# A hidden layer of gates as a block product of seven parts

## The chip, the cores and the metric

The kernel runs on one core of a Trainium2 chip. The metric is the device time of one execution in microseconds, here the median of the runs shown; one execution was also taken by the profiler, with its own time.

## The reference

Two layers over 512 latent tokens of width 1024, in float32, with 256 context tokens beside them in the first layer. Each layer normalizes, modulates with a scale and a shift made from a conditioning vector, mixes tokens, projects back and adds a gated residual. The first mixer is a bidirectional gated recurrence of 16 heads of 128 channels:

```python
    p = (h @ w_in).reshape(B, N, HG_STREAMS, HG_HEADS, HG_HEAD_DIM)
    q = jax.nn.silu(p[0])
    f = lbh + (1.0 - lbh) * jax.nn.sigmoid(p[1:3].astype(jnp.float32))
    return q, 1.0 - f, jnp.log(f), p[3], p[4]
```

So a head has five streams: a query, two forget gates (one for each direction), a value and a gate path. The context goes through the same weights and gives the state with which the latent recurrence of each direction starts; of a context token only the gates and the value are needed. The second mixer is a Fourier transform over tokens and channels, with its own gate path. A last normalization ends it.

## The kernel before

A product in float32 is made of three matmuls on rounded parts: `mm3` multiplies high by high, high by low and low by high. The parts of the tokens (`hlh`, `hll` for latent, `hc` for context, 8 blocks of 128 channels each) are made once. Those of the weights are made as they arrive: `split` copies the high part on ScalarE (ACT, L56, `wh`) and subtracts it on VectorE (DVE, L57, `wl`). The class `Weights` keeps three raw tiles of 512 KB (`wr`, fetched by SyncE, SP) and three of each part, and works one piece ahead of the product.

A head's streams 1 and 2 are the gates, 0 the query and 3 the gate path. `proj` makes for each gate 24 matmuls of 512 latent columns (`pf`) and 24 of 256 context columns (`pfc`), then 24 of 512 for the query and 24 for the path (both `pq`). The gate's sigmoid and its scale run on ACT (L455, L456), its complement goes to the tile `z` (L466). `proj_v` makes the values of two heads (`vps`, matmuls of 256 columns). The program goes through eight pairs: `proj` of the even head, `proj_v`, `proj` of the odd head.

Beside it runs the recurrence of the head before (`scan`): seven levels that double the span. At each level after the first, four matmuls `gp` (L578, eight with both passes of float32) go from `z` and its copy `kk` into PSUM; DVE multiplies `z` twice by the decays (L586), ACT makes the next `kk` (L545), and DVE copies the masked scores (L605). The next `gp` needs this `kk`. After the levels come the states, the read-out, its normalization (POOL, GpSimd) and the head's output `y`, kept in SBUF (`py`). `advance` runs one piece of a scan at each yield of the projections, and from step 30 on every third step runs a piece of the side work `ada_rest`: 32 loads of 512 KB (`ar`, two buffers, the next requested ahead of the use) that DVE accumulates (L401) into rows, from which come the second layer's modulation and two residual gates (`gates`, in SBUF).

Inside the startup the order of PE, ACT and DVE is that of the program (`manual_schedule`); POOL and SP are free. For each of eight blocks d it makes modulation columns (`rp`, `row` on ACT, then the matmul `mp`), transposes the latent tokens, modulates them into `hlh` and `hll`, and runs products of head 0 between. Then it does the same for the context. Everywhere else a scheduler sets each engine's order, by priorities that follow the program and by the buffers that come free. At the end the output product of the first layer takes `y` of all heads (`out0_early`, `out0_late`), and the second layer follows.

## Time and profile before

| | us |
|---|---|
| median of the runs (lowest, highest) | 1210.17 (1208.92, 1210.5) |
| profiled execution | 1208.84 |
| its span, first to last instruction | 1207.0 |
| TensorE (PE) busy | 1186.8 (98%) |
| VectorE (DVE) busy | 763.6 (63%) |
| ScalarE (ACT) busy | 562.6 (47%) |
| GpSimd (POOL) busy | 42.8 (4%) |

The mean granted TensorE clock is 0.995. "PEld" is the weight load, which runs beside the matmuls. In a group's row stand the line, engine, operation, output and inputs with their shapes, then the count, busy time, the mean of one in ns, and the engine's idle time before them with what ended it. In a timeline's row the first two numbers are start and length in us.

### The profile page before, as it was taken

The numbers are of one execution on the slowest core, as the hardware profiler recorded it, in microseconds if no ns is written. First come the engines' busy times: TensorE is split into PE (matmuls) and PEld (weight loads), VectorE is DVE, ScalarE is ACT, GpSimd is POOL, SyncE is SP. The second block draws the span as 40 slices with busy tenths as digits, with TensorE's granted clock in tenths as the row PEclk, the third lists the DMA queues.
The fourth block names the chain that finished last, engine by engine and source line by source line (L and its number), as shares of the span: only waits on it lengthen the run. The fifth ranks groups of instructions, "written<-read, shape, count | busy, mean of one in ns | idle before, by whom it ended". The sixth has DMA issues, their size and how long they took to land.

```text
span 1207.0 us, 18983 instructions
## 1 busy us (share of the span) xinstructions
PE 1186.8 (98%) x7677; PEld 1050.8 (87%) x7677; DVE 763.6 (63%) x1250; ACT 562.6 (47%) x1130; POOL 42.8 (4%) x76
## 2 busy tenths in 40 slices
...
GB/s 358 183 123 141 71 53 53 53 71 70 168 59 31 174 78 53 71 140 71 36 70 53 35 54 70 37 53 107 163 179 182 111 43 134 108 108 120 88 87 70
DMA packets 33673, 118.52 MB, mean 98 GB/s; under 512 B 3879, under 2 KB 4144, under 8 KB 33586
## 3 DMA queue, kind: packets, MB, share of 16 engines
...
## 4 chain that ended last, share of the span: by engine, by line
PE 90%; DVE 4%; DMA 2%; ACT 2%; issue 1%; POOL 1%; SPq 0%; DVEq 0%; POOLq 0%; ACTq 0%
PE gp L578 7%; PE pf L95 4%; PE pq L95 4%; PE pq L97 4%; PE pq L96 4%; PE pf L97 4%; PE pf L96 4%; PE vps L95 4%; PE vps L96 4%; PE vps L97 4%; PE pfc L95 2%; PE pfc L96 2%; PE pfc L97 2%; PE o0a L97 2%; PE o0a L95 2%; PE o0a L96 2%
## 5 line engine op out<-in xcount | busy, mean ns | idle before, releaser
L56 ACT ACTIVATE wh<-wr 128x1024 fp32r<-128x1024 f32 x140 | 148.0, 1058 | 229.9 <-PE pq L96 89.3
L57 DVE TENSOR_TENSOR wl<-wr,wh 128x1024 fp32r<-128x1024 f32 x140 | 170.7, 1220 | 100.4 <-ACT wh L56 100.2
L586 DVE TENSOR_TENSOR z<-z,tt 128x512 f32<-128x512 f32 x192 | 124.0, 687 | 122.3 <-PE gp L578 110.9
L578 PE MATMUL gp<-z,kk 128*128 128x128 f32 x768 | 103.5, 277 | 0.7 <-ACT kk L545 0.6
L578 PEld LDWEIGHTS gp<-z,kk 128*128 128x128 f32 x768 | 97.6, 191 | 6.7 <-ACT kk L545 3.3
L95 PE MATMUL pf<-hlh,wh 128*128 128x512 f32 x240 | 99.2, 413 | 0.0
L95 PE MATMUL pq<-hlh,wh 128*128 128x512 f32 x240 | 97.1, 405 | 0.0
L545 ACT ACTIVATE kk<-z 128x512 f32<-128x512 f32 x96 | 61.8, 644 | 71.5 <-DVE z L586 71.3
L97 PE MATMUL pf<-hlh,wl 128*128 128x512 f32 x240 | 94.5, 394 | 0.0
L97 PE MATMUL pq<-hlh,wl 128*128 128x512 f32 x240 | 93.9, 391 | 0.0
L96 PE MATMUL pf<-hll,wh 128*128 128x512 f32 x240 | 93.7, 391 | 0.0
L96 PE MATMUL pq<-hll,wh 128*128 128x512 f32 x240 | 93.5, 390 | 0.0
L95 PE MATMUL pfc<-hc,wh 128*128 128x256 f32 x256 | 74.8, 292 | 0.0
L95 PE MATMUL vps<-wh,hlh 128*128 128x256 f32 x256 | 74.2, 291 | 0.0
L97 PE MATMUL vps<-wh,hll 128*128 128x256 f32 x256 | 72.6, 283 | 0.0
L96 PE MATMUL vps<-wl,hlh 128*128 128x256 f32 x256 | 72.5, 283 | 0.0
L96 PE MATMUL pfc<-hc,wh 128*128 128x256 f32 x256 | 72.4, 283 | 0.0
L97 PE MATMUL pfc<-hc,wl 128*128 128x256 f32 x256 | 72.4, 283 | 0.0
L97 PEld LDWEIGHTS pf<-hlh,wl 128*128 128x128 f32 x240 | 45.0, 188 | 10.4 <-issue 0.2
L97 PEld LDWEIGHTS pq<-hlh,wl 128*128 128x128 f32 x240 | 45.1, 188 | 10.0
L95 PEld LDWEIGHTS pf<-hlh,wh 128*128 128x128 f32 x240 | 45.2, 188 | 9.5 <-issue 1.9
L96 PEld LDWEIGHTS pf<-hll,wh 128*128 128x128 f32 x240 | 45.3, 189 | 8.2 <-issue 0.2
...
## 6 DMA issues: line engine op xcount, KB each, us to landing
wr<-hg_w SPq DMA_DIRECT2D x64, 512.0 KB, 3.5
ar<-ada_r SPq DMA_DIRECT2D x32, 512.0 KB, 3.8
wr<-ft_w SPq DMA_DIRECT2D x32, 512.0 KB, 4.0
wr<-hg_wout SPq DMA_DIRECT2D x29, 512.0 KB, 3.5
wa<-ada_a SPq DMA_DIRECT2D x16, 512.0 KB, 10.5
wr<-hg_v SPq DMA_DIRECT2D x16, 512.0 KB, 3.4
wr<-ft_wout SPq DMA_DIRECT2D x16, 512.0 KB, 3.5
xs<-x SPq DMA_DIRECT2D x4, 512.0 KB, 3.7
```

What stands on the lines that cost most here:

```text
L56: s.activation(hi, src, AF.Copy)
L57: v.tensor_tensor(out=lo, in0=src, in1=hi.bitcast(F32), op=ALU.subtract)
L95: pe.matmul(out, lh, rh, start=first, stop=False)
L96: pe.matmul(out, lh, rl, start=False, stop=False)
L97: pe.matmul(out, ll, rh, start=False, stop=last)
L545: s.activation(view(kk, 0, [[2 * h, T // (2 * h)], [h, 2], [1, h]]), view(z4, 2 * T, [[2 * h, T // (2 * h)], [T + h, 2], [1, h]]), AF.Copy)
L578: pe.matmul(gp[:, n * P:(n + 1) * P], kk[:, n * P:(n + 1) * P], view(z4, n * P, dims), start=True, stop=True)
L586: v.tensor_tensor(out=za, in0=za, in1=ta, op=ALU.mult)
```

## The change

The 2048 columns that a head's two gates make (two streams, latent and context) become one product of a weight matrix and a token matrix, each cut two by two. Weights are cut by stream and by half of the 1024 input channels, tokens by half of the channels and by even and odd blocks of 128 tokens (384 of the 768). Seven products of sums replace eight:

- `mixes` makes the four token sums with four dependent subtractions and additions on POOL for each k (256 latent columns, later 128 context columns), and splits each into high and low parts (ACT and DVE). This stands in the startup: latent k = 0 to 3 after the blocks d = 4 to 7, context after d = 5 and 7 of the context. The modulated tokens are written back into `xs` for it. The casts and sums of the masks on POOL now stand inside the startup too, and the mask tile has four planes.
- `fold_piece` makes the seven weight pieces of 128 x 512 out of the two streams' raw tiles, four of them by a DVE operation in place. Each is split.
- In `proj`, for heads 1 to 15, `prod` runs 12 matmuls of 384 columns for each piece (`px`). Five sums on DVE, two copies on ACT and two additions on POOL put the results together, and sigmoid and gate run on all 768 columns at once. Head 0 is as before.

To make room, the outputs `y` of heads 0 to 12 go to DRAM (`yd`) and come back in halves (`yr`) for the output product; the two residual gates go there as rows (`grow`) and come back broadcast. The side work's `ar` has one buffer, and the next load is requested behind the use of the one before.

```diff
--- before.py
+++ after.py
...
+    pd = ctx.enter_context(tc.tile_pool(name="pd", bufs=1, space=bass.MemoryType.DRAM))
...
-                if j == 3:
-                    hi, lo = (py.tile(shape, F32R, tag=f"yp{6 + b}", name=f"wz{b}") for b in range(2))
+                if j in pieces:
+                    both = pw.tile([P, 2, KT // 2, P], F32R, tag="wh" if pieces[j] % 2 else "wl", name=f"wp{j}")
+                    hi, lo = both[:, 0], both[:, 1]
+                elif j == 3:
+                    hi, lo = (p0.tile(shape, F32R, tag=f"junk{b}", name=f"wz{b}") for b in range(2))
...
-            self.halves(n + 1)
+            self.halves(n + 3 if n in pieces and pieces[n] < 4 else n + 1)
...
-        h32 = p0.tile([P, T], F32, tag="h32", name=f"h32_{d}_{e}", bufs=2)
+        h32 = xs[:, n0:n1, d * P:(d + 1) * P]
+        t3 = tp[:, :w].rearrange("p (n c) -> p n c", c=P)
...
+    def mixes(k0, k1, e):
+        m, n0 = ((2, 0), (1, NT))[e]
+        xt = xs.rearrange("p n (h k c) -> p h k n c", h=2, c=P)
+
+        def part(kh, half, k):
+            return xt[:, kh, k, n0 + half:n0 + half + 2 * m - 1:2, :]
+
+        for t in range(4):
+            if mix[t] is None:
+                mix[t] = [ph.tile([P, KT // 2, N // 2], F32R, tag=f"t{2 * t + b}", name=f"mix{t}_{b}") for b in range(2)]
+        for k in range(k0, k1):
+            b11, b12, b21, b22 = (part(kh, half, k) for kh in range(2) for half in range(2))
+            g.tensor_tensor(out=b22, in0=b22, in1=b12, op=ALU.subtract)
+            g.tensor_tensor(out=b12, in0=b12, in1=b11, op=ALU.subtract)
+            g.tensor_tensor(out=b11, in0=b22, in1=b11, op=ALU.add)
+            g.tensor_tensor(out=b21, in0=b21, in1=b11, op=ALU.subtract)
+            for t, src in ((2, b22), (0, b12), (1, b11), (3, b21)):
+                c = slice(0, 2 * P) if e == 0 else slice(2 * P, 3 * P)
+                hi, lo = (mix[t][b][:, k, c].rearrange("p (n c) -> p n c", c=P) for b in range(2))
+                split(hi, lo, src)
...
+    def fold_piece(w, j):
+        p = pieces[j]
+        w.loaded(j - p + 1)
+        f1, f2 = w.raw[j - p], w.raw[j - p + 1]
+        a11, a12, a21, a22 = f1[:, :4], f1[:, 4:], f2[:, :4], f2[:, 4:]
+        if p == 2:
+            v.tensor_tensor(out=a21, in0=a21, in1=a22, op=ALU.add)
+            v.tensor_tensor(out=a11, in0=a21, in1=a11, op=ALU.subtract)
+        elif p == 4:
+            v.tensor_tensor(out=a21, in0=a22, in1=a11, op=ALU.subtract)
+        elif p == 5:
+            v.tensor_tensor(out=a12, in0=a12, in1=a11, op=ALU.subtract)
+        return (a11, a12, a11, a21, a21, a12, a22)[p]
+
+    def head_specs(i):
+        if i == 0:
+            for st in (1, 2):
+                spec(("w", i, st), a["hg_w"][i, st], [P, KT, P])
+        else:
+            for p in range(7):
+                pieces[len(specs)] = p
+                spec(("f", i, p), a["hg_w"][i, 1 + p] if p < 2 else None, [P, KT, P], fold_piece)
+        for st in (0, 3):
+            spec(("w", i, st), a["hg_w"][i, st], [P, KT, P])
...
-            if d == 6:
-                W.halves(3)
+            if d >= KT // 2:
+                mixes(d - 4, d - 3, 0)
+        W.halves(3)
         for j in range(3):
             product(j, KT - 2)
         for n in range(NT, NT + NTC):
             normalize(n)
         for j in range(3):
             product(j, KT - 1)
+        g.tensor_copy(masks, mraw[:, 1:])
+        for t, src in ((own_m, ident), (near_m, mraw[:, 0, :])):
+            msum = p0.tile([P, 32], F32, tag="msum", name=f"msum{t.name}", bufs=2) if t is near_m else own_m
+            g.tensor_tensor(out=msum, in0=src[:, 0:32], in1=src[:, 32:64], op=ALU.add)
+            for j in (64, 96):
+                g.tensor_tensor(out=msum, in0=msum, in1=src[:, j:j + 32], op=ALU.add)
+            if t is near_m:
+                g.tensor_copy(near_m, msum)
...
+            if d in (5, 7):
+                mixes(d - 5, d - 3, 1)
...
+    yd = [pd.tile([P, T], F32, name=f"yd{i}") for i in range(13)]
...
-                raw = sp.tile([P, D], F32, tag="ar", name=f"ar{j}_{k}", bufs=2)
+                raw = sp.tile([P, D], F32, tag="ar", name=f"ar{j}_{k}")
...
-                fetch()
...
+                fetch()
...
-                    s.activation(gates[0 if j == 0 else 1][:, h * 512:(h + 1) * 512], q, AF.Copy)
+                    s.activation(acc[0:1, h * 512:(h + 1) * 512], q[0:1, :], AF.Copy)
+                nc.sync.dma_start(out=grow[0 if j == 0 else 1], in_=acc[0:1, :])
...
+        def out(st, half):
+            return ff[:, 2 - st].rearrange("p (n e c) -> p e n c", e=2, c=P)[:, half]
+
+        def tri(t):
+            return t[:, :nh].rearrange("p (n c) -> p n c", c=P)
+
+        def prod(p, rhs):
+            acc = psP(f"px{i}_{p}")
+            hi, lo = W.get(base + p)
+            for k in range(KT // 2):
+                mm3(tri(acc), hi[:, k, :], lo[:, k, :], rhs(0, k), rhs(1, k), k == 0, k == KT // 2 - 1)
+            return acc
+
+        def block(kh, half):
+            return lambda b, k: tiled[b][:, kh * 4 + k, half]
+
+        def mixed(t):
+            return lambda b, k: mix[t][b][:, k, :].rearrange("p (n c) -> p n c", c=P)
+
+        def kept(acc, name):
+            c = sp.tile([P, nh], F32, tag="cc", name=f"{name}{i}", bufs=2)
+            s.activation(c, acc[:, :nh], AF.Copy)
+            return c
+
+        def add(eng, dst, x, y):
+            eng.tensor_tensor(out=dst, in0=x, in1=y, op=ALU.add)
+
+        u = kept(prod(0, block(0, 0)), "u")
+        yield None
+        add(v, out(1, 0), tri(prod(1, block(1, 0))), tri(u))
+        yield None
+        add(v, u, prod(2, mixed(1))[:, :nh], u)
+        yield None
+        c5 = kept(prod(3, mixed(0)), "c5")
+        add(g, out(1, 1), tri(u), tri(c5))
+        yield None
+        add(v, u, prod(4, mixed(2))[:, :nh], u)
+        add(g, out(2, 1), tri(u), tri(c5))
+        yield None
+        add(v, out(1, 1), tri(prod(5, block(1, 1))), out(1, 1))
+        s.activation(ff[:, 1, :], ff[:, 1, :], AF.Sigmoid)
+        gate(1)
+        yield None
+        add(v, out(2, 0), tri(prod(6, mixed(3))), tri(u))
+        s.activation(ff[:, 0, :], ff[:, 0, :], AF.Sigmoid)
+        gate(2)
+        yield None
         for st, dst in ((0, q), (3, zs)):
...
+        y = py.tile([P, T], F32, tag="y" if i < LAST else f"y{i}", name=f"y{i}")
         v.scalar_tensor_tensor(out=y, in0=tp, scalar=ngc, in1=zs, op0=ALU.mult, op1=ALU.mult)
+        if i < LAST:
+            nc.sync.dma_start(out=yd[i], in_=y)
...
+    def y_fetch(k, r, ahead):
+        n = back[r].index((k, r))
+        for kk, _ in back[r][:n + 1 + ahead]:
+            if (kk, r) not in got:
+                t = got[kk, r] = (fp if r else sp).tile([P, 256], F32, tag="yr" if r else "cc", name=f"yr{r}_{kk}",
+                                                        bufs=3 if r else 2)
+                nc.sync.dma_start(out=t, in_=yd[kk][:, r * 256:(r + 1) * 256])
+        return got[k, r]
+
+    def y_parts(k, r, late=True):
+        y2 = (fp if late else sp).tile([P, 2, 256], F32R, tag="o0y" if late else "q", name=f"o0y{r}_{k}", bufs=2)
+        src = ys[k][:, r * 256:(r + 1) * 256] if k >= LAST else y_fetch(k, r, 2 if late else 1)
+        split(y2[:, 0], y2[:, 1], src)
...
+    for j in range(2):
+        gates[j] = fp.tile([P, D], F32, tag=f"gate{j}", name=f"gate{j}")
+        nc.sync.dma_start(out=gates[j], in_=grow[j].broadcast_to([P, D]))
```

In the startup, ACT, around the blocks d = 4 and 5 (`hlh` is the modulated block, `row` the copy of the next block's modulation row, `mix` the high parts of the token sums, `xs` the modulated block in float32). Before:

```order
L238 ACTIVATE hlh<-tp_0_378,bcol,acol 128x512
L215 ACTIVATE row_410<-rp_401 128x256
L238 ACTIVATE hlh<-tp_0_416,bcol,acol 128x512
L241 ACTIVATE h_5_0_436<-tp_0_416,bcol,acol 128x512
L215 ACTIVATE row_448<-rp_439 128x256
```

and in the change:

```order
L250 ACTIVATE hlh<-tp_0_376,bcol,acol 128x512
L58 ACTIVATE mix_0_402<-xs 128x256
L58 ACTIVATE mix_0_398<-xs 128x256
L58 ACTIVATE mix_0_400<-xs 128x256
L58 ACTIVATE mix_0_404<-xs 128x256
L227 ACTIVATE row_427<-rp_418 128x256
L250 ACTIVATE hlh<-tp_0_433,bcol,acol 128x512
```

Four copies of sums stand between a block's modulation and the next block's row.

In the pairs, DVE, at the levels of head 13 beside the gates of head 14 (`z` multiplications by `tt`, masked copies `am`, weight splits `wl` and `wp`, sums of the products `px`). Before:

```order
L586 TENSOR_TENSOR z_13_6571<-z_13_6571,tt_0_6908 128x2x128x2 x2
L605 COPY_PREDICATED am_6882<-masks,gp_1_6925 128x512
L586 TENSOR_TENSOR z_13_6571<-z_13_6571,tt_1_6935 128x2x64x4 x2
L605 COPY_PREDICATED am_6882<-masks,gp_2_6968 128x512
L57 TENSOR_TENSOR wl_7087<-wr_6865,wh_7086 128x1024
L513 SCALAR_TENSOR_TENSOR rr<-fc_6858,ones 128x255
L586 TENSOR_TENSOR z_13_6571<-z_13_6571,tt_2_6978 128x2x32x8 x2
L605 COPY_PREDICATED am_6882<-masks,gp_3_6999 128x512
L586 TENSOR_TENSOR z_13_6571<-z_13_6571,tt_3_7009 128x2x16x16 x2
L605 COPY_PREDICATED am_6882<-masks,gp_4_7032 128x512
```

and in the change:

```order
L686 TENSOR_TENSOR z_13_6871<-z_13_6871,tt_0_7214 128x2x128x2 x2
L705 COPY_PREDICATED am_7188<-masks,gp_1_7234 128x512
L574 TENSOR_TENSOR u_7184<-px_2_7250,u_7184 128x384
L59 TENSOR_TENSOR wl_7382<-wr_7318,wh_7381 128x1024
L686 TENSOR_TENSOR z_13_6871<-z_13_6871,tt_1_7244 128x2x64x4 x2
L705 COPY_PREDICATED am_7188<-masks,gp_2_7268 128x512
L686 TENSOR_TENSOR z_13_6871<-z_13_6871,tt_2_7278 128x2x32x8 x2
L705 COPY_PREDICATED am_7188<-masks,gp_3_7299 128x512
L574 TENSOR_TENSOR u_7184<-px_4_7317,u_7184 128x384
L59 TENSOR_TENSOR wl_7422<-wr_7347,wh_7421 128x1024
L686 TENSOR_TENSOR z_13_6871<-z_13_6871,tt_3_7309 128x2x16x16 x2
```

A sum of a product and a split now stand between the masked copy and the next multiplication at every second level.

In the side work, DVE, at one of its groups (`acc` accumulates `ar`). Before, with the multiplications of head 4:

```order
L399 TENSOR_SCALAR acc_2867<-ar_0_2600,scol 128x1024
L401 SCALAR_TENSOR_TENSOR acc_2867<-ar_1_2868,scol,acc_2867 128x1024
L586 TENSOR_TENSOR z_4_2186<-z_4_2186,tt_5_2859 128x2x4x64 x2
L401 SCALAR_TENSOR_TENSOR acc_2867<-ar_2_2976,scol,acc_2867 128x1024
L401 SCALAR_TENSOR_TENSOR acc_2867<-ar_3_3073,scol,acc_2867 128x1024
L57 TENSOR_TENSOR wl_3047<-wr_2831,wh_3046 128x1024
L401 SCALAR_TENSOR_TENSOR acc_2867<-ar_4_3124,scol,acc_2867 128x1024
L513 SCALAR_TENSOR_TENSOR rr<-fc_2824,ones 128x255
L401 SCALAR_TENSOR_TENSOR acc_2867<-ar_5_3251,scol,acc_2867 128x1024
```

and in the change, with those of head 6:

```order
L461 TENSOR_SCALAR acc_3822<-ar_0_3678,scol 128x1024
L686 TENSOR_TENSOR z_6_3303<-z_6_3303,tt_1_3806 128x2x64x4 x2
L705 COPY_PREDICATED am_3743<-masks,gp_2_3848 128x512
L463 SCALAR_TENSOR_TENSOR acc_3822<-ar_1_3941,scol,acc_3822 128x1024
L686 TENSOR_TENSOR z_6_3303<-z_6_3303,tt_2_3858 128x2x32x8 x2
L705 COPY_PREDICATED am_3743<-masks,gp_3_3885 128x512
L463 SCALAR_TENSOR_TENSOR acc_3822<-ar_2_4062,scol,acc_3822 128x1024
L686 TENSOR_TENSOR z_6_3303<-z_6_3303,tt_3_3895 128x2x16x16 x2
L705 COPY_PREDICATED am_3743<-masks,gp_4_3928 128x512
```

Three accumulations, each of a load that is requested behind the one before, stand between level multiplications; before, only the last multiplication had any of the group ahead of it.

164 lines of the change are left out of this document (76 added, 88 removed).

## The prediction

> **What bounds the kernel now.** I read the page's first part and its chain of waits, then the stretches of the span, then the timeline.
>
> ```profile
> PE 1186.8 (98%) x7677; PEld 1050.8 (87%) x7677; DVE 763.6 (63%) x1250; ACT 562.6 (47%) x1130; POOL 42.8 (4%) x76
> PE 90%; DVE 4%; DMA 2%; ACT 2%; issue 1%; POOL 1%; SPq 0%; DVEq 0%; POOLq 0%; ACTq 0%
> ```
>
> TensorE (PE) is busy for 98% and the chain runs on it for 90%: a matmul removed is time gained, as long as nobody else becomes late. The stretches say where somebody could (columns: stretch, its length, busy time and instructions of PE, PEld, DVE, ACT, POOL, the granted clock, DMA share, GB/s):
>
> ```profile
> 20.00:30.00 10.00, 8.07 (x50) 5.12 (x43) 4.90 (x10) 4.77 (x7) 0.00 (x0) 0.74 1.03 410
> 50.00:60.00 10.00, 7.33 (x36) 5.00 (x34) 7.25 (x14) 4.55 (x7) 4.88 (x8) 1.00 0.42 139
> 70.00:80.00 10.00, 10.00 (x92) 9.29 (x91) 10.00 (x17) 5.47 (x11) 0.00 (x0) 1.00 0.34 105
> 230.50:329.50 99.00, 98.65 (x663) 88.88 (x662) 65.29 (x103) 49.18 (x107) 2.86 (x4) 1.00 0.30 96
> 626.60:725.70 99.10, 99.10 (x682) 89.87 (x682) 58.24 (x99) 48.19 (x105) 2.40 (x4) 1.00 0.18 57
> ```
>
> The last two are pairs of heads: PE never stops, VectorE (DVE) has 58 of 99 us, 65 where the side work runs. The first three belong to the startup: PE has holes, and just after it DVE is full.
>
> **Gate matmuls (A).** Starts of neighbours give the pitch: 22 intervals of 512 columns between the first two rows, 22 of 256 between the last two.
>
> ```profile
> 421.87 0.39 PE L96 MATMUL pq<-hll,wh 128*128 128x512 f32 x1
> 426.86 0.39 PE L97 MATMUL pq<-hlh,wl 128*128 128x512 f32 x1
> 399.88 0.28 PE L96 MATMUL pfc<-hc,wh 128*128 128x256 f32 x1
> 402.51 0.28 PE L97 MATMUL pfc<-hc,wl 128*128 128x256 f32 x1
> ```
>
> That is 0.2268 and 0.1195 us. A head's gates were 48 of 512 and 48 of 256 columns, 16.62 us; now 7 products x 4 blocks x 3 = 84 of 384 columns. No row has 384; I take the middle, 0.1732, 14.55 us. So 2.07 us less for each of 15 heads: **-31.1 us**. Bounds: priced as 256 columns -98.7, as 512 columns +36.4.
>
> **What that costs the other engines in the pairs (B).** The groups:
>
> ```profile
> L57 DVE TENSOR_TENSOR wl<-wr,wh 128x1024 fp32r<-128x1024 f32 x140 | 170.7, 1220 | 100.4 <-ACT wh L56 100.2
> L57 DVE TENSOR_TENSOR o1y<-yf,o1y 128x512 fp32r<-128x512 f32 x16 | 10.9, 681 | 0.0
> L473 DVE TENSOR_TENSOR q<-pq,q 128x512 f32<-128x512 f32 x15 | 10.2, 683 | 0.0
> L57 DVE TENSOR_TENSOR u<-up,u 128x258 fp32r<-128x258 f32 x16 | 6.7, 418 | 0.0
> L56 ACT ACTIVATE wh<-wr 128x1024 fp32r<-128x1024 f32 x140 | 148.0, 1058 | 229.9 <-PE pq L96 89.3 <-issue 53.3 <-PE zp L96 25.4
> L56 ACT ACTIVATE o1y<-yf 128x512 fp32r<-128x512 f32 x16 | 9.9, 620 | 3.2 <-DVE u L57 2.8 <-PE dp L97 0.4
> L455 ACT ACTIVATE fl<-pf 128x512 f32<-128x512 f32 x30 | 17.9, 598 | 54.9 <-PE pf L97 54.8
> L455 ACT ACTIVATE fc<-pfc 128x256 f32<-128x256 f32 x32 | 11.8, 374 | 0.0
> L456 ACT ACTIVATE fl<-fl,lbc,omlb 128x512 f32<-128x512 f32 x32 | 26.0, 815 | 1.0
> L456 ACT ACTIVATE fc<-fc,lbc,omlb 128x256 f32<-128x256 f32 x32 | 19.1, 599 | 0.5
> ```
>
> DVE per head: two weight splits of 1024 go (-2.44), seven of 512 come (7 x 0.681 = 4.77), four folds (4 x 0.683 = 2.73), five adds of 384 columns (between 0.418 and 0.683, say 0.55: 2.75). Together +7.8, so a pair has 58 + 16 = 74, with side work 81, in the 95 us that PE leaves: 78% and 85%. ScalarE (ACT): seven copies of 0.620 for two of 1.058 (+2.2), two copies of 384 columns near 0.49, and the four gate steps on 768 columns (0.82 and 1.03 by the lines through 256 and 512) for eight (4.77 to 3.70, -1.1): +2.1, 52 of 95 us. Two additions per head go to GpSimd (POOL), beside other work.
>
> DVE is not full, so the cost is a loop. Levels of the recurrence run beside the products:
>
> ```profile
> 433.36 1.12 PE L578 MATMUL gp<-z,kk 128*128 128x128 f32 x8
> 434.23 0.38 PE L95 MATMUL pfc<-hc,wh 128*128 128x256 f32 x1
> 434.60 1.29 DVE L586 TENSOR_TENSOR z<-z,tt 128x512 f32<-128x512 f32 x2 [2.98 <-PE gp L578]
> 435.81 0.73 DVE L605 COPY_PREDICATED am<-masks,gp 128x512 f32<-128x512 uint8 x1
> 435.92 0.63 ACT L545 ACTIVATE kk<-z 128x512 f32<-128x512 f32 x1 [0.25 <-DVE z L586]
> ```
>
> One level's matmul at 433.36 makes the next possible at 435.92 + 0.63 = 436.55: 3.19 us round. PE had 0.87 (433.36 to 434.23) plus twelve matmuls of 512 or 24 of 256 columns to issue meanwhile, 3.6 to 3.7 us, so DVE sat waiting (the 2.98). Beside an odd head's levels PE now has one product, 0.87 + 12 x 0.1732 = 2.95 us: the round no longer fits and PE waits 0.24 us at each of six levels, 1.44 a pair. Three of these rounds have a copy (0.73), an addition (0.55) and a split of 1024 (1.22) in DVE's row between two multiplications (1.29): 3.79, or 0.84 late; but the rounds between them have only the copy and can make that up. So 1.4 for each of some 7 pairs that have both: **+10 us**. Bounds: 0 if products of which PE already has the operands lie ahead of the late level; 3 x 0.84 + 3 x 0.24 = 3.24 a pair, +24, if nothing is made up. I take the bare round, since the additions can slip behind the multiplications.
>
> **One buffer for the side work (C).**
>
> ```profile
> ar<-ada_r SPq DMA_DIRECT2D x32, 512.0 KB, 3.8
> L401 DVE SCALAR_TENSOR_TENSOR acc<-ar,scol,acc 128x1024 f32<-128x1024 f32 x30 | 38.4, 1280 | 10.0 <-DMA ar<-ada_r 9.9
> ```
>
> With two buffers the next load ran beside the accumulation and DVE still waited 9.9 us for loads. With one, a step takes 3.8 + 1.28 = 5.1 us. Three of the accumulations of each later group stand in DVE's row between level multiplications, beside PE rounds of 3.7 us: 3 x 1.4 = 4.2 per group, less the slack with which the first of them begins, about 3, for the three groups after the startup: **+9 us**. Head weights queue on SP behind these loads, with two to three tiles ahead to cover it. Bounds: 0 if DVE gets early, +27 if all seven reloads of a group count in full.
>
> **Startup (D).** Here ACT and DVE keep the written order, and PE was back to back:
>
> ```profile
> 40.90 0.50 PE L221 MATMUL mp<-sel,row 128*128 128x2 f32 x4
> 44.90 0.50 PE L221 MATMUL mp<-sel,row 128*128 128x2 f32 x4
> 38.45 0.38 ACT L215 ACTIVATE row<-rp 128x256 f32<-128x256 f32 x1
> 38.58 0.81 DVE L243 TENSOR_SCALAR h<-tp,acol,bcol 128x512 f32<-128x512 f32 x1 [0.91 <-ACT hlh L238]
> 2.69 0.25 POOL L361 TENSOR_TENSOR own_m<-ident 128x32 f32<-128x32 f32 x1 [1.62 <-DMA ident<-ident]
> 49.06 0.41 POOL L179 TENSOR_SCALAR rstd_x<-ss 128x1 f32<-128x1 f32 x1 [35.10 <-ACT junk L201]
> 51.32 0.55 POOL L180 TENSOR_TENSOR rstd_x<-rstd_x,nhalf 128x1 f32<-128x1 f32 x1
> 52.47 1.47 POOL L358 CAST masks<-mraw 128x896 uint8<-128x896 f32 x1 [0.60 <-DMA mraw<-masks]
> 53.91 0.69 POOL L361 TENSOR_TENSOR msumnear_m<-mraw 128x32 f32<-128x32 f32 x1
> L56 ACT ACTIVATE o0y<-y 128x256 fp32r<-128x256 f32 x32 | 13.2, 413 | 16.1 <-PE o0a L97 14.9 <-DVE y L656 1.1
> ```
>
> The block for d = 4 cannot start before h is written (38.58 + 0.81 = 39.4). It is four dependent POOL operations of 256 columns. Their price is not in the trace. The 32-column row and the cast differ by 864 columns and 1.22 us: 1.41 ns a column, 0.57 us for 256; a second input at the same rate again gives 0.88. I take 0.75, nearer the upper end, as each operation reads two tiles. The last ACT copy of the four then ends at 39.4 + 3.0 + 0.41 = 42.8, and only behind it stands the copy of the next `row`, at 38.45 before; the matmul `mp` that needs it moves from 40.90 to 43.2, +2.3. For d = 5 the same 2.3 and, between its links on POOL, the moved cast (512 columns, 0.9) and sums (three of 0.25): +3.9. For d = 6 the first again, with `h` on DVE, +2.6. After d = 7 the context's statistics (49.06 to 51.87, 2.8 on POOL) and the last chain stand before DVE's normalization: +5.6. The transposes of the context begin 14 us later. Then context blocks of 128 columns, copies that delay the first context gates, and a DVE that was full from 70 us on: +4. Together **+18 us**. The prices of 0.57 and 0.88, over 16 links of 256 columns and 16 shorter ones, move it by some 4 either way: 14 and 22; and 10 if the last 4 are hidden too.
>
> [...]
>
> A chain stretched this far leaves PE holes of 6 us and more. What a slow clock costs is in two rows, the same sixteen matmuls:
>
> ```profile
> 25.66 1.93 PE L213 MATMUL rp<-wa,spad 128*32 128x256 f32 x16
> 33.15 1.07 PE L213 MATMUL rp<-wa,spad 128*32 128x256 f32 x16
> ```
>
> Twice the time, in the stretch whose granted clock was 0.74. I add nothing, and up to 3 us to the upper bound. [...]
>
> **DRAM for outputs and gates (E).** Thirteen writes and 26 fetches on SP, far from the end; the fetches are requested one or two steps ahead of use, a step of the output product is at least 12 x 0.2268 = 2.7 us, and a load four times their size took 3.8. **0**, -1 to +3.
>
> **Sum.** -31.1 + 10 + 9 + 18 + 0 = +5.9, on the profiled execution's 1208.84 (span 1207.0 and 1.84 around it): 1214.7. The median of the runs is 1.3 above that execution: **1216**.
>
> **Rivals.**
>
> R1, faster: DVE keeps pace. If products and banks let PE run ahead and the side work's reload falls into DVE's free 15 to 20%, B is 1 and C 2; it decides as long as DVE's row is empty when a level's matmul ends, as the 2.98 us wait above says it was. For it: 15% free. Against it: the round of 3.19 is longer than 2.95. Time: 1210.2 - 31.1 + 1 + 2 + 18 = 1200; with POOL operations at 0.57, 1196.
>
> R2, DVE is the bound in the pairs: B +24, C +15, D +18: 1210.2 - 31.1 + 57 = 1236. For it: 85% on paper, and no round made up; against: copies and additions can wait.
>
> R3, POOL and DVE hold each other up. The 32-column sum took 0.69 beside DVE's normalization and 0.25 alone, +0.44. If half of the 16 latent links pay that, the startup grows by 3.5; the 30 additions in the pairs, of about 1 us each on POOL, can stop a late level multiplication for as long: if every fourth does, +8. 1216 + 11.5 = 1228. [...]
>
> R4, the change doesn't save: 384 columns in blocks cost what 512 do: 1216 + 67 = 1283.
>
> **How the numbers follow.** Forecast 0.49, R1 0.33, R2 0.08, R3 0.08, R4 0.02. About 0.2%, 2.4 us, is what a measurement of this kernel can tell from no change. The forecast's own range is 1208 to 1227: 0.37 slower, 0.10 same, 0.02 faster. R1 is 0.30 faster, 0.03 same. So faster 0.32, same 0.13, slower 0.55. R1 reaches from 1190 to 1208, two thirds of it above 1196; R3 and half of R2 end below 1236: with the range 1196 to 1236 under 2 in 10 is left out.
>
> **What would show it.** Starts of neighbouring `px` matmuls 0.173 us apart (A); PE idle of over 1 us in a pair, ended by ACT `kk` or DVE `z` (B); in three pairs several us more, DVE waiting for `ar` (C); context transposes some 14 us later, after waits for `row` and the normalized `xs` (D). Wrong if pairs take 95 us without idle (R1) or the startup moves by under 10 us.

## The result

The changed kernel takes **1231.1 us** (median of 4 runs, 1230.1 to 1231.6) against 1210.3 for the kernel before: a ratio of 1.0172, interval 1.0154 to 1.0190. It is 20.7 us slower where 5.8 was forecast. The sign was right and the time lies in the range, but most of the loss was not foreseen.

The same lines of the page as were shown of before, now of the changed kernel:

```profile
PE 1182.0 (96%) x7497; PEld 1054.5 (86%) x7497; DVE 880.9 (72%) x1492; ACT 600.6 (49%) x1205; POOL 104.4 (8%) x138
PE 72%; DVE 12%; ACT 8%; POOL 3%; issue 3%; DMA 2%; SPq 0%; DVEq 0%; POOLq 0%; ACTq 0%
```

TensorE's busy time fell by only 4.8 us although matmuls worth 31 by the forecast's count went away. The rows that stay are longer (a level matmul `gp` 283 ns in the mean, before 277), so busy time doesn't measure what was saved. The chain that sets the end left TensorE: 72% of the span instead of 90%. VectorE, ScalarE and GpSimd have 23% together, before 7%.

Where in the span, the starts of two matmuls tell: the first `vps` of the first pair of heads (end of the startup) and that of the last pair. Before:

```profile
69.97 0.28 PE L95 MATMUL vps<-wh,hlh 128*128 128x256 f32 x1
766.35 0.36 PE L95 MATMUL vps<-wh,hlh 128*128 128x256 f32 x1
```

and in the change:

```profile
93.55 0.39 PE L103 MATMUL vps<-wh,hlh 128*128 128x256 f32 x1 [0.53 <-ACT ff L533]
785.62 0.28 PE L103 MATMUL vps<-wh,hlh 128*128 128x256 f32 x1
713.15 0.34 PE L104 MATMUL px<-hll,wp 128*128 128x384 f32 x1
714.88 0.33 PE L105 MATMUL px<-hlh,wp 128*128 128x384 f32 x1
```

The last two are ten intervals apart: 0.173 us for 384 columns, as the sum had it. At this pitch the matmuls saved are the 2.07 us a head that the forecast counted. The table takes this count, and by it the difference of the profiled spans (1229.1 - 1207.0 = 22.1 us) divides so:

| stretch | before | after | matmuls saved | so lost | forecast |
|---|---|---|---|---|---|
| startup, to the first `vps` | 69.97 | 93.55 | 0 | +23.6 | D +18 |
| seven pairs, first `vps` to last | 696.4 | 692.1 | -29.0 | +24.7 | B + C +19 |
| last pair to the end | 440.6 | 443.5 | -2.1 | +4.8 | E 0 |
| sum | | | -31.1 | +53.1 = +22.0 net | +37 = +5.9 net |

The pairs, in the stretches view (stretch, length, busy time and instructions of PE, PEld, DVE, ACT, POOL, granted clock, DMA share, GB/s), the first and third without side work, the second with it:

```profile
192.00:288.60 96.60, 95.80 (x653) 88.76 (x652) 71.14 (x125) 51.79 (x112) 8.29 (x8) 1.00 0.18 61
288.60:388.90 100.30, 97.85 (x657) 89.45 (x656) 80.45 (x133) 52.58 (x114) 8.81 (x8) 1.00 0.31 100
689.00:785.60 96.60, 95.79 (x653) 88.71 (x652) 71.00 (x125) 51.77 (x112) 8.28 (x8) 1.00 0.18 61
```

A pair without side work took 98.1 before (668.24 to 766.35) and takes 96.64 between its `vps` starts: 1.5 faster where the matmuls alone give 4.14. The missing 2.65, seven times, is 18.6 of the 24.7; the other four pairs, the first one among them, have the side work and lose about 6.0 more between them. VectorE is full in none of them: 71 of 96.6, 80 of 100.3.

Startup, the chain behind the block d = 4 (GpSimd's sums, then ScalarE, then the matmul `mp` of the next block):

```profile
39.35 0.81 DVE L256 TENSOR_SCALAR xs<-tp,acol,bcol 128x512 f32<-128x512 f32 x1 [0.91 <-ACT hlh L250]
40.20 0.69 DVE L258 TENSOR_TENSOR hll<-xs,hlh 128x512 fp32r<-128x512 f32 x1
41.03 0.74 POOL L273 TENSOR_TENSOR xs<-xs 128x256 f32<-128x256 f32 x1 [26.28 <-DVE hll L258]
41.85 0.73 POOL L274 TENSOR_TENSOR xs<-xs 128x256 f32<-128x256 f32 x1
42.65 0.78 POOL L275 TENSOR_TENSOR xs<-xs 128x256 f32<-128x256 f32 x1
43.52 0.79 POOL L276 TENSOR_TENSOR xs<-xs 128x256 f32<-128x256 f32 x1
44.34 0.42 ACT L58 ACTIVATE mix<-xs 128x256 fp32r<-128x256 f32 x1 [0.45 <-POOL xs L276]
44.66 0.36 ACT L227 ACTIVATE row<-rp 128x256 f32<-128x256 f32 x1
45.08 0.61 PE L233 MATMUL mp<-sel,row 128*128 128x2 f32 x4 [3.24 <-ACT row L227]
53.36 0.61 PE L233 MATMUL mp<-sel,row 128*128 128x2 f32 x4 [2.42 <-ACT row L227]
61.05 0.61 PE L233 MATMUL mp<-sel,row 128*128 128x2 f32 x4 [3.42 <-ACT row L227]
```

The forecast's order of events is there link by link, with `row` last, and a GpSimd operation of 256 columns costs 0.73 to 0.79 us where 0.75 was taken. What it had wrong is the start: the first sum overwrites a block of `xs` in place, and VectorE still reads that block for `hll`, so the chain begins at 41.03 and not at 40.16 (39.35 + 0.81), when the block is written. In before the four `mp` of d = 4 to 7 stood at 36.73 to 48.89, 12.2 us; now they stand at 37.50 to 61.05, 23.6 us. That is +11.4 where 8.8 was forecast.

### The profile page after: what moved, and what is told of

Read it like the earlier page. It is cut to its first block, busy times and chain, and to the rows that moved or that the text cites. A ratio compares the mean times of both kernels' runs of the same rounds, so it can differ in the third digit from the quotient of the medians.

```text
span 1229.1 us, 19234 instructions
## 1 busy us (share of the span) xinstructions
PE 1182.0 (96%) x7497; PEld 1054.5 (86%) x7497; DVE 880.9 (72%) x1492; ACT 600.6 (49%) x1205; POOL 104.4 (8%) x138
## 4 chain that ended last, share of the span: by engine, by line
PE 72%; DVE 12%; ACT 8%; POOL 3%; issue 3%; DMA 2%; SPq 0%; DVEq 0%; POOLq 0%; ACTq 0%
PE gp L678 5%; DVE z L686 4%; PE px L103 4%; PE px L104 4%; PE px L105 3%; PE pq L105 3%; PE pq L104 3%; PE pq L103 3%; PE vps L103 3%; PE vps L105 3%; PE vps L104 3%; PE o0a L105 2%; PE o0a L103 2%; PE o0a L104 2%; PE o1a L103 2%
## 5 line engine op out<-in xcount | busy, mean ns | idle before, releaser
L103 PE MATMUL vps<-wh,hlh 128*128 128x256 f32 x384 | 112.8, 294 | 0.5 <-ACT ff L533 0.5
L105 PE MATMUL vps<-wh,hll 128*128 128x256 f32 x384 | 109.9, 286 | 0.0
L58 ACT ACTIVATE wp<-wr 128x512 fp32r<-128x512 f32 x105 | 65.0, 627 | 82.4 <-PE pq L104 73.5
L574 POOL TENSOR_TENSOR ff<-u,c 128x384 f32<-128x384 f32 x30 | 45.4, 1515 | 492.5 <-ACT c L570 408.9
L59 DVE TENSOR_TENSOR wp<-wr,wp 128x512 fp32r<-128x512 f32 x105 | 71.0, 686 | 20.1 <-ACT wp L58 19.8
L103 PE MATMUL px<-mix,wp 128*128 128x384 f32 x240 | 84.4, 352 | 0.0
L104 PE MATMUL px<-mix,wp 128*128 128x384 f32 x240 | 82.1, 342 | 0.0
L105 PE MATMUL px<-mix,wp 128*128 128x384 f32 x240 | 81.3, 339 | 0.0
L103 PEld LDWEIGHTS vps<-wh,hlh 128*128 128x128 f32 x384 | 73.7, 192 | 2.8 <-issue 2.1
L104 PEld LDWEIGHTS vps<-wl,hlh 128*128 128x128 f32 x384 | 73.8, 192 | 0.7 <-issue 0.5
L105 PEld LDWEIGHTS vps<-wh,hll 128*128 128x128 f32 x384 | 73.8, 192 | 0.6 <-issue 0.6
L103 PE MATMUL px<-hlh,wp 128*128 128x384 f32 x180 | 62.3, 346 | 0.0
```

The lines of the kernel that those rows point to most:

```text
L58: s.activation(hi, src, AF.Copy)
L59: v.tensor_tensor(out=lo, in0=src, in1=hi.bitcast(F32), op=ALU.subtract)
L103: pe.matmul(out, lh, rh, start=first, stop=False)
L104: pe.matmul(out, lh, rl, start=False, stop=False)
L105: pe.matmul(out, ll, rh, start=False, stop=last)
L574: eng.tensor_tensor(out=dst, in0=x, in1=y, op=ALU.add)
```

## The experiments

Two theories on the startup: **chain** (GpSimd's dependent sums delay `row` and later the context) and **clock** (the holes in PE lower its clock, and that costs the time). Three on the pairs: **load** (VectorE has too much), **hold-up** (GpSimd's additions and VectorE's operations stop each other, rival R3), **order** (short waits behind ScalarE's and VectorE's rows, for which PE no longer has work ahead). Ratios are against the kernel before, run on the same chip; the change has 1.0172. The medians of the kernel before lie between 1208.7 and 1210.3 on these chips, so a difference of two experiments' times is good to 1 or 2 us.

**The splits of the sums written later.** The sums on GpSimd stay in place; the ScalarE copies and VectorE subtractions behind them come a block or more later in the rows, so that `row` isn't behind them.

```diff
+            if d > 5:
+                mixes(d - 6, d - 5, 0, 2)
...
-                mixes(d - 4, d - 3, 0)
+                mixes(d - 4, d - 3, 0, 1)
...
+        mixes(2, 3, 0, 2)
...
-                mixes(d - 5, d - 3, 1)
+                mixes(d - 5, d - 3, 1, 1)
+            if d == 7:
+                mixes(0, 2, 1, 2)
+    mixes(2, 4, 1, 2)
```

> The change with only the order of the token sums in the startup altered: the POOL operations stay where they are in the program, but the copies and splits of a block's sums come two blocks later, behind the copy of the next row; those of the last context blocks come behind the written order. Same work. Theory 'chain': the startup lost 23.6 us (first matmul of the values at 93.55 us, before 69.97) because each row copy and the context's normalization stood behind four dependent POOL operations, and because the holes lowered the clock. Then the values start at 74 to 82 us and the run takes 1214 to 1220 us. Rival 'work': 32 more copies on ScalarE, 32 more splits on VectorE and hold-ups between POOL and VectorE cost that time wherever they stand: values at 88 us or later, 1226 us or more.

1222.2 us, ratio 1.0111 (1.0096 to 1.0126). The first `vps` comes at 81.85 instead of 93.55, and the first pair gives 2.9 of that back:

```profile
81.85 0.58 PE L103 MATMUL vps<-wh,hlh 128*128 128x256 f32 x1 [4.31 <-ACT ff L543]
```

The same operations, in another place of two in-order rows, are worth 8.9 us, and the four late `mp` stand within 12.2 us again (35.60 to 47.79), as in the kernel before. That is the chain, though the run ends 2 us later than the expectation allowed; what is left waits at the end of the startup, for the first gate.

**No sums.** The four GpSimd operations of each `mixes` are left out, so the products take unsummed token blocks; all splits and all matmuls stay.

```diff
-            g.tensor_tensor(out=b22, in0=b22, in1=b12, op=ALU.subtract)
-            g.tensor_tensor(out=b12, in0=b12, in1=b11, op=ALU.subtract)
-            g.tensor_tensor(out=b11, in0=b22, in1=b11, op=ALU.add)
-            g.tensor_tensor(out=b21, in0=b21, in1=b11, op=ALU.subtract)
```

> The change without the 32 POOL operations of the token sums: the copies and splits stay in their places and split the modulated blocks themselves, so the sums are left out of the computation. 'Chain': the waits of PE for the row copies (3.24, 2.42, 3.42 us) and for the normalized context (4.12) nearly vanish, what stays is about 1.7 us of copies per block: values start at 74 to 80 us, 1212 to 1218 us. 'Work': 86 us or later, 1224 us or more.

1211.1 us, ratio 1.0014 (1.0005 to 1.0023):

```profile
75.58 0.38 PE L103 MATMUL vps<-wh,hlh 128*128 128x256 f32 x1
```

Of the 23.6 us, 18.0 go at the first `vps` with 32 GpSimd operations; the 32 splits that remain cost 5.6. So D is, for the most part, the time of those operations in a chain, and the pairs (691.5) don't move.

**Additions on VectorE.** The two additions per head go from GpSimd to VectorE, which is a test of hold-up against load: load predicts slower, hold-up faster.

```diff
-        add(g, out(1, 1), tri(u), tri(c5))
+        add(v, out(1, 1), tri(u), tri(c5))
...
-        add(g, out(2, 1), tri(u), tri(c5))
+        add(v, out(2, 1), tri(u), tri(c5))
```

> The change with the two additions per head moved from POOL to VectorE (0.55 to 0.6 us each there, 1.5 us on POOL). The pairs without side work took 96.6 us, 2.7 more than PE's own 93.9. Theory 'hold-up': POOL's additions stop the level multiplications (some took 0.9 to 1.05 us instead of 0.65): a pair gets 0.5 to 1 us shorter, the run 1224 to 1228 us. Theory 'load': VectorE's row is what is late, and 2.3 us more in it per pair make a pair 0.3 to 1.5 us longer: 1233 to 1242 us. Theory 'PE': the pairs' loss is PE's own changes between kinds of matmuls and waits for ScalarE: within 0.3 us a pair, 1229 to 1233 us.

1226.5 us, ratio 1.0141 (1.0124 to 1.0158). The pairs' sum falls from 692.1 to 687.6: more work on VectorE, and less time. The groups say why (count, then busy us and mean ns of one); first the change:

```profile
L574 POOL TENSOR_TENSOR ff<-u,c 128x384 f32<-128x384 f32 x30 | 45.4, 1515 | 492.5 <-ACT c L570 408.9 <-DVE st L731 36.7 <-DVE z L686 25.0
L686 DVE TENSOR_TENSOR z<-z,tt 128x512 f32<-128x512 f32 x192 | 130.3, 721 | 69.5 <-PE gp L678 67.9 <-ACT ff L589 1.0 <-ACT st L634 0.3
```

then the experiment:

```profile
L686 DVE TENSOR_TENSOR z<-z,tt 128x512 f32<-128x512 f32 x192 | 124.0, 689 | 64.0 <-PE gp L678 63.4 <-ACT st L634 0.6
L574 DVE TENSOR_TENSOR ff<-u,c 128x384 f32<-128x384 f32 x30 | 16.7, 555 | 4.7 <-ACT c L570 4.3
```

An addition takes 1.52 us on GpSimd in the mean and 0.56 on VectorE, and the level multiplications are back from 721 to 689 ns (687 before the change). In the change's timeline, an addition alone, and one that begins just behind a weight split of VectorE, with the level multiplications that follow:

```profile
726.32 1.00 POOL L574 TENSOR_TENSOR ff<-u,c 128x384 f32<-128x384 f32 x1 [34.85 <-ACT c L570]
...
364.67 1.21 DVE L59 TENSOR_TENSOR wl<-wr,wh 128x1024 fp32r<-128x1024 f32 x1
364.76 2.00 POOL L574 TENSOR_TENSOR ff<-u,c 128x384 f32<-128x384 f32 x1 [2.30 <-DVE tt L707]
365.81 2.11 DVE L686 TENSOR_TENSOR z<-z,tt 128x512 f32<-128x512 f32 x2
```

Alone an addition takes 1.00. The second one begins 0.09 after the split does and ends 0.88 after it, so it takes 2.00. The pair of multiplications begins beside it and takes 2.11 where 1.29 is usual, 1.50 of it in the first of the two. So hold-up is shown, both ways: of all 224 level multiplications eight take 1.2 to 1.5 us and the others 0.72 at most, and each of the eight stands beside an addition. Without it the pairs are 4.4 us shorter, 3.9 of them in the three later pairs with side work (two faster by 2.5, one slower by 1.1). The size is less certain than the cause: in other runs here whose pairs have the change's instructions the pairs' sum was 691.5 to 694.4, so the gain is 3.9 to 6.8.

**No folds.** The four VectorE operations that add weight pieces are left out (the products take unsummed pieces), 2.7 us less VectorE work per head.

```diff
-        if p == 2:
-            v.tensor_tensor(out=a21, in0=a21, in1=a22, op=ALU.add)
-            v.tensor_tensor(out=a11, in0=a21, in1=a11, op=ALU.subtract)
-        elif p == 4:
-            v.tensor_tensor(out=a21, in0=a22, in1=a11, op=ALU.subtract)
-        elif p == 5:
-            v.tensor_tensor(out=a12, in0=a12, in1=a11, op=ALU.subtract)
```

> The change without the four folds of weight pieces per head (2.73 us of VectorE per head, 5.5 per pair; the pieces are split unfolded, so the products are of other weights). 'Load': with so much less in VectorE's row a pair loses 1 to 2 of its 2.7 us, the run takes 1215 to 1223 us. 'Hold-up' and 'PE': under 0.5 us a pair, 1227 to 1231 us.

1230.3 us, ratio 1.0177 (1.0156 to 1.0198): nothing. Pairs without side work take 96.73 and 96.70 instead of 96.64. Load falls, and with it the mechanism of R2, as far as the folds stand for VectorE's work.

**One buffer for `ar`, in the kernel before.** This is C alone.

```diff
-                raw = sp.tile([P, D], F32, tag="ar", name=f"ar{j}_{k}", bufs=2)
+                raw = sp.tile([P, D], F32, tag="ar", name=f"ar{j}_{k}")
...
-                fetch()
                 yield
...
+                fetch()
```

> The kernel before with the side work's one load buffer alone: one `ar` tile, the next load requested behind the use of the one before. The prediction's term for this was +9 us (a step of 3.8 + 1.28 = 5.1 us beside level rounds of 3.7): 1216 to 1222 us if it holds. Rival, from the trace of the change (there the accumulations waited 1.3 us and less, off the path, since a level round with an accumulation is about 4.4 us and hides a load of 3.5): within 1.5 us of 1209.7.

1209.8 us, ratio 1.0002 (0.9992 to 1.0012). In this kernel C is nothing, where +9 was forecast; the experiment with all moves below says the same of the changed one.

**Outputs and gates in DRAM, in the kernel before.** This is E alone.

```diff
+    yd = [pd.tile([P, T], F32, name=f"yd{i}") for i in range(13)]
...
+        if i < LAST:
+            nc.sync.dma_start(out=yd[i], in_=y)
...
+        src = ys[k][:, r * 256:(r + 1) * 256] if k >= LAST else y_fetch(k, r, 2 if r else 1)
```

> The kernel before with the outputs of heads 0 to 12 and the residual gates kept in DRAM alone, fetched back as in the change. The change's tail, from the output product to the end, was 4 us longer: the output product 1.1 us, the second layer 2.8 us, with the 512-column matmuls of its gate path 0.233 us apart instead of 0.228. Theory 'transfers': the fetches and the gates are what costs: 1212 to 1214 us. Rival 'placement': the pitch depends on where the tiles lie, the transfers cost nothing: 1209 to 1211 us, with a pitch that may be either.

1209.6 us, ratio 1.0000 (0.9991 to 1.0009). The transfers are hidden, as forecast; the 4.8 us behind the last pair have another cause.

**The gates' second step on VectorE.** One 1.02 us row of ScalarE per gate goes to VectorE.

```diff
-            s.activation(ff[:, 2 - st, :], ff[:, 2 - st, :], AF.Identity, scale=omlb[:, col:col + 1], bias=lbc[:, col:col + 1])
+            v.tensor_scalar(out=ff[:, 2 - st, :], in0=ff[:, 2 - st, :], scalar1=omlb[:, col:col + 1], scalar2=lbc[:, col:col + 1],
+                            op0=ALU.mult, op1=ALU.add)
```

> The change with the gate's scale and offset (768 columns, 1.03 us on ScalarE, twice per head) on VectorE. In a pair without side work PE's waits add up to 2.3 us: 0.72 for the transposes `ktp` behind the copy `st`, 0.59 behind the read-out `os`, about 1 for `gp` behind `kk`, all on ScalarE. Theory 'ScalarE': its row is what is late, and 2 us less per head make a pair 0.7 to 1.8 us shorter: 1218 to 1226 us. Theory 'VectorE': its row is, and a pair gets longer by 1 us or more: 1236 us or later. Within 0.3 us a pair would say that neither row's length matters, only the order.

1226.3 us, ratio 1.0134 (1.0118 to 1.0151); pairs 688.5, so 3.6 less, a pair without side work 96.2: 0.4 less, which lies between what the expectation gave for ScalarE's row and for the order alone. What moved is a wait that the change's timeline shows in six of the seven pairs:

```profile
770.88 1.02 ACT L519 ACTIVATE ff<-ff,lbc,omlb 128x768 f32<-128x768 f32 x1
773.09 0.28 ACT L635 ACTIVATE st<-s 128x128 f32<-128x128 f32 x1
773.42 0.55 PE L722 MATMUL ktp<-ident,z 128*128 128x128 f32 x3 [0.55 <-ACT st L635]
```

and the groups of the matmuls that depend on such rows. In the kernel before:

```profile
L578 PE MATMUL gp<-z,kk 128*128 128x128 f32 x768 | 103.5, 277 | 0.7 <-ACT kk L545 0.6
L622 PE MATMUL ktp<-ident,z 128*128 128x128 f32 x96 | 13.1, 272 | 0.0
```

in the change:

```profile
L678 PE MATMUL gp<-z,kk 128*128 128x128 f32 x768 | 107.7, 283 | 5.7 <-ACT kk L644 4.9
L722 PE MATMUL ktp<-ident,z 128*128 128x128 f32 x96 | 14.7, 276 | 3.4 <-ACT st L635 3.4
```

and in this experiment:

```profile
L679 PE MATMUL gp<-z,kk 128*128 128x128 f32 x768 | 106.7, 282 | 7.8 <-ACT kk L645 7.1
L723 PE MATMUL ktp<-ident,z 128*128 128x128 f32 x96 | 14.1, 276 | 0.0
764.32 0.28 ACT L635 ACTIVATE st<-s 128x128 f32<-128x128 f32 x1
767.95 0.81 PE L723 MATMUL ktp<-ident,z 128*128 128x128 f32 x6
```

The level matmuls `gp` were busy for 4.2 us more and waited 5.0 more with the change, `ktp` 1.6 and 3.4, over all 16 heads. Moving one ScalarE row takes the wait of `ktp` away: ScalarE's copy `st` now stands well ahead of it (764.32), while `gp` waits 2.1 longer. VectorE got more work, so it isn't VectorE's load, but what stands in ScalarE's row ahead of `st`. That row also got shorter, so this run doesn't part its order from its length.

What the 24.7 us of the pairs are, PE's rows tell when they are counted from start to start between the first and the last `vps`, with an idle time given to the row behind it: `gp` 7.9, `ktp` 3.1, the read-out's transposes `otp` 3.7, the query and path matmuls 3.0, `vps` 2.8, the rest 0.6. The last 3.6 were never saved: the gate products took 243.5 us before and 218.1 now, 25.4 less where the table counts 29.0. A part of that is the switch between products: a first `px` behind a matmul of another kind mostly stands 0.26 us ahead of the next one, and not 0.17. No run tells the causes of the other rows apart.

**Both repairs.** Splits later in the rows, the context's sums spread over its blocks with half of its float32 copies on ScalarE, additions on VectorE:

```diff
-        if e == 0 and d % 2:
+        if d % 2:
...
+            if d > 5:
+                mixes(d - 6, d - 5, 0, 2)
...
-            if d in (5, 7):
-                mixes(d - 5, d - 3, 1)
+            if d >= 4:
+                mixes(d - 4, d - 3, 1, 1)
+            if d >= 6:
+                mixes(d - 6, d - 5, 1, 2)
...
-        add(g, out(1, 1), tri(u), tri(c5))
+        add(v, out(1, 1), tri(u), tri(c5))
```

> Two of the moves together, further: the token sums' splits a block later than in the first experiment, the context's sums one block at a time with the odd blocks modulated on ScalarE, and the additions of each head on VectorE. By 'chain' and 'hold-up' the startup ends (first matmul of the values) at 76 to 80 us and the pairs save 4 us: 1212 to 1217 us. If the first experiment already took all that order can give: 1217 to 1219.

1213.2 us, ratio 1.0028 (1.0017 to 1.0040): first `vps` at 80.44 after a wait of 3.82 us for the first gate, pairs 688.0. The gains of the first and the third experiment (8.9 and 4.6) add up, and 4.4 more come, with the context's sums spread: the first `vps` is 1.4 earlier than with the late splits alone, and the first pair takes 98.9 where that one took 101.4.

**All of it.** To the last one come the gate step on VectorE, the first head weights split ahead of the last sums, another PSUM bank for the first `vps` (so that PE has work while the context's splits run), and the output stage's pools in another order (below).

```diff
+    W.halves(5)
     mixes(2, 4, 1, 2)
...
-            ps_ = psP(f"vps{pr}_{m}")
+            ps_ = (psM if pr == 0 and m == 0 else psP)(f"vps{pr}_{m}")
...
-    fp = ctx.enter_context(tc.tile_pool(name="fp", bufs=1))
     ph = ctx.enter_context(tc.tile_pool(name="ph1", bufs=1))
+    fp = ctx.enter_context(tc.tile_pool(name="fp", bufs=1))
```

> All moves together: the later token sums and the additions on VectorE of the experiment before, the gate's scale and offset on VectorE, the split of the first value weights ahead of the last token sums, the first value product in another PSUM bank (it waited 3.8 us for a bank that the late sigmoids of head 0 held), and the second layer's `ph1` pool placed ahead of `fp`. If the terms add: 1213.2 less 4 (gates), less 3 (startup), less 2 if the 0.233 us pitch of the second layer's gate path comes from where its tiles lie: 1203 to 1208 us, faster than both kernels. If VectorE, which now carries sums and gates, becomes late in the pairs: 1210 to 1216 us.

**1205.2 us, ratio 0.9963 (0.9951 to 0.9976)**: faster than both kernels, by 0.37% against before. The second pair begins at 174.0 (before 168.6, the change 192.0), so of the startup's loss 5.5 us remain, counted at the second pair, and a pair without side work takes 95.94 us:

```profile
173.98:269.92 95.94, 95.56 (x653) 88.81 (x653) 75.10 (x135) 48.21 (x108) 2.41 (x4) 1.00 0.21 67
```

The seven products do pay once the rows around them are rearranged: 26 of the 53 us lost are got back, with VectorE at 75 of 96 us and GpSimd at 2.4. No run makes these moves in the kernel before, but there PE waited for only 1.1 us in all seven pairs, so little could be won in them. The side work still has its one buffer: the three later pairs with it lose 1.6 to 2.0 us beside the matmuls saved, those without it 1.9 to 2.2. So C is nothing here too.

**PE kept busy in the holes.** Ten matmuls of ones ahead of each late `mp` and fourteen ahead of the context, to test clock.

```diff
+            if d > 4:
+                fill(10, f"fill{d}")
             ada_cols(d)
...
+        fill(14, "fill8")
```

> The change with 44 matmuls of ones (512 columns, 0.23 us each, results unused) in the startup's holes of PE: ten ahead of each `mp` of d = 5, 6 and 7, fourteen ahead of the context's transposes. They fit inside the waits of 3.24, 2.42, 3.42 and 4.12 us. Theory 'clock': of the startup's 23.6 us some 18.6 are idle time and some 4.8 are matmuls at half clock behind the holes; with the holes filled the clock stays up and 2 to 5 us return: 1226 to 1229 us. Rival: the low clock comes by chance or costs nothing on the path: 1230 to 1232 us.

1235.0 us, ratio 1.0218 (1.0202 to 1.0233), and no answer: the fill took the PSUM bank from which ScalarE had yet to copy `row`, so the first of its matmuls waited for the same chain, and all of them then stood ahead of `mp`:

```profile
44.20 0.50 PE L151 MATMUL fill<-ones_r 128*128 128x512 f32 x1 [3.23 <-ACT row L232]
```

**The holes filled with products by zero.** Eleven matmuls that add zero to a sum already open, which wait for nothing.

```diff
+            if d > 4:
+                for j in range(11):
+                    pe.matmul(first[FIRST[0]], zero_r, hlh[:, 0, :T], start=False, stop=False)
             ada_cols(d)
```

> The change with eleven more matmuls of 512 columns ahead of each `mp` of d = 5, 6 and 7; they multiply block 0 by a tile of zeros into an accumulator that PE is filling anyway, so they wait for nothing but PE. (In the tenth experiment the filling matmuls themselves waited 3.23 us for the row copy that they were to cover.) 11 x 0.23 = 2.5 us fits the waits of 3.24, 2.42 and 3.42 us; the holes ahead of the context's transposes and gates stay. Theory 'clock': no low clock from 40 to 70 us, 1 to 3 us return: 1228 to 1230 us. Rival: chance, or free: 1230.5 to 1232 us, and 1232 or more if the filling itself stands in the way.

1230.6 us, ratio 1.0176 (1.0154 to 1.0197). The granted clock in the change, first between the `mp` of d = 5 and of d = 6, then in the context's part, and below it the experiment between the same `mp` and between those of d = 6 and d = 7:

```profile
45.00:53.30 8.30, 5.86 (x33) 3.88 (x33) 3.68 (x10) 3.40 (x8) 4.61 (x8) 0.79 0.01 3
70.00:80.00 10.00, 7.99 (x31) 6.00 (x32) 8.92 (x16) 3.96 (x7) 0.14 (x1) 0.67 0.33 105
80.00:90.00 10.00, 6.55 (x35) 5.72 (x35) 6.89 (x20) 5.45 (x17) 7.08 (x16) 0.84 0.01 2
```

```profile
43.40:51.40 8.00, 6.78 (x44) 5.00 (x44) 4.35 (x10) 3.37 (x7) 4.16 (x9) 1.00 0.00 1
51.40:59.70 8.30, 8.22 (x44) 6.40 (x45) 4.89 (x10) 3.30 (x8) 3.07 (x4) 0.79 0.00 0
```

Between the `mp` of d = 5 and of d = 6 the change has a clock of 0.79 and takes 8.28 us (45.08 to 53.36); with full clock the experiment takes 8.05 (43.43 to 51.48). So the clock is 0.2 us of that block at most, and GpSimd's chain the rest. A full clock from 40 to 70 us, as the expectation had it, did not come: in the next block the experiment has 0.79, behind holes of PE of 1.3 us and less, and there `mp` stood behind the products by zero (8.24 for 7.69). So the four late `mp` take 23.9 us (35.82 to 59.72) against 23.6. The context's part, where the granted clock is 0.67 to 0.84, was not filled, so that what a slow clock costs there stays open, within the 7.0 us by which this part is longer.

**The output stage's pools in another order.** Only where tiles lie in SBUF changes; no instruction does.

```diff
-    fp = ctx.enter_context(tc.tile_pool(name="fp", bufs=1))
     ph = ctx.enter_context(tc.tile_pool(name="ph1", bufs=1))
+    fp = ctx.enter_context(tc.tile_pool(name="fp", bufs=1))
```

> The change with the second layer's `ph1` pool placed ahead of `fp` alone, so that only where tiles lie in SBUF differs. Theory 'placement': the 512-column matmuls of the second layer's gate path return from 0.233 to 0.228 us apart, 312 x 0.0055 = 1.7 us: 1228.5 to 1230 us. Rival: something else among the moves of the ninth experiment did it: pitch 0.233, 1230.5 to 1232 us.

1231.0 us, ratio 1.0184 (1.0167 to 1.0201): the time does not move, but one pitch does. First and last of 23 neighbours of the 512-column matmuls `zp`, in the change:

```profile
1039.96 0.40 PE L104 MATMUL zp<-h1l,wh 128*128 128x512 f32 x1
1045.10 0.40 PE L105 MATMUL zp<-h1h,wl 128*128 128x512 f32 x1
```

and in the experiment:

```profile
1039.24 0.39 PE L103 MATMUL zp<-h1h,wh 128*128 128x512 f32 x1
1044.28 0.39 PE L104 MATMUL zp<-h1l,wh 128*128 128x512 f32 x1
```

5.14 us against 5.04 for 22 intervals: 0.2336 and 0.229, the latter near before's 0.228. Over the 312 matmuls of the stage it is 1.7 us. The stages ahead of it lost most of that again: the output product 0.8, the part between it and the gate path 0.6. So placement explains the pitch, and 1.7 of the tail's 4.8. By the starts of the stages 0.9 more lie in the last pair itself and 1.1 in the output product, which stay open; another 0.9 lie in the Fourier part ahead of the gate path, which took 1.4 longer in the kernel before with one `ar` buffer than without that edit, by the same instructions.

## Why the prediction was right, and where it was wrong

**A, right in the pitch.** "I take the middle, 0.1732": 0.173 was measured, and R4 is out. Of the 29.0 us that this gives for the seven pairs, PE's rows show 25.4: what the start of a product costs behind another kind of matmul was no term.

**B, mis-sized: +10 forecast, 24.7 in all.** "1.4 for each of some 7 pairs" was 2.65 a pair, and 6.0 more beside the side work. The step that failed is "So 1.4": it priced one loop, the round of the level multiplications, as the only work that PE runs out of cover for. The loop itself was sized about right: `gp` with its waits for `kk` (0.7 us before, 5.7 now) is 7.9 us of the seven pairs, 1.1 a pair. What the sum had at nothing are `ktp` behind `st` on ScalarE (no wait before, 3.4 now), the read-out's `otp` (3.7), the longer rows of the other products (5.8) and the 3.6 that A lacks. The experiment on the gate step shows the wait of `ktp`; the others were only counted. Bounds of 0 and 24 were given (3.24 for each of seven pairs is 22.7); the truth lies at the upper one, but not by "nothing is made up", since the loop cost 1.1 a pair and not 3.24.

**R3, given 0.08, was a part of it.** Hold-up costs 4.4 us in the pairs where +8 was worked out for it, shown by moving the additions. POOL's 1.00 us becomes 1.5 in the mean and 2.0 just behind a split, and the first multiplication that begins beside that addition takes 1.50 where 0.69 is the median. What the two engines stop each other on, no run shows.

**C, wrong: +9 forecast, 0 measured.** The step that failed is "Three of the accumulations ... stand in DVE's row between level multiplications, beside PE rounds of 3.7 us". With an accumulation in it a round is longer than that:

```profile
312.86 1.28 DVE L463 SCALAR_TENSOR_TENSOR acc<-ar,scol,acc 128x1024 f32<-128x1024 f32 x1
317.72 1.28 DVE L463 SCALAR_TENSOR_TENSOR acc<-ar,scol,acc 128x1024 f32<-128x1024 f32 x1
323.22 1.28 DVE L463 SCALAR_TENSOR_TENSOR acc<-ar,scol,acc 128x1024 f32<-128x1024 f32 x1 [1.34 <-DMA ar<-ada_r]
ar<-ada_r SPq DMA_DIRECT2D x32, 512.0 KB, 3.5
```

The first two are 4.9 us apart with no wait: the round is longer by the accumulation itself, and a load of 3.5 fits behind it. Before the third VectorE does wait, 1.34 us, but the same single buffer cost nothing in the kernel before, and nothing with all moves. A wait of an engine that is not the bound was priced as time. Of the 6.0 us that the pairs with side work lose beyond the others, the additions on VectorE gave 3.9 back.

**D, right in kind, short by 5.6.** The chain was told in its order, the price of a GpSimd operation was right, and removing these operations gave 20.0 us back. Two terms were mis-sized. Between the late `mp`: 11.4 for 8.8, because the sums overwrite a block that `hll` still reads, and each link of the chain has a gap of about 0.1. In the context, "+4" was 7.0: sixteen short links of 0.45 to 0.55 us, and about a third of the first head's 48 context gate matmuls (between 86.7 and 90.2 us) at a pitch of 0.21 us for 256 columns instead of 0.12 (by these rows an estimate of 1.5 us). "I add nothing" for the clock held between two of the late `mp`, where full clock was worth 0.2 us. In the change a low clock follows the holes of 3.2 to 4.1 us (0.79 from 45.00 to 53.30 and from 61.00 to 69.00, 0.67 from 70 to 80, 0.84 from 80 to 90) and none follows that of 2.4 (1.00 from 53.30 to 61.00). Two other stretches have a low clock without such a hole: the zero products' 0.79 came behind holes of 1.3 us and less, and the stretch of 0.74 (20 to 30 us, before) has none above 1.41. From what length on a hole would lower the clock, no run shows.

**E, right for the transfers, wrong for the stage.** They cost nothing, alone in the kernel before. That the change also moves tiles, and that a pitch hangs on where they lie (1.7 us), was no term; what else the stage lost has no cause shown.

**Sum.** Of the 16.1 us between forecast and span, 5.7 come from the pairs (B +14.7, C -9), 5.6 from the startup, 4.8 from the tail. R1, at 0.33, was wrong as the change is written; the last rearrangement ends near its 1200, by other terms: 5.5 us of the startup (R1 had 18) and 2.0 in each pair (R1 had 1 in all).
